# Dilated 3x3 convolution: TensorE's third to eighth pair of images as a loop of six turns, and a smaller tail of the last load in five transfers

## The chip, the cores and the metric

The kernel runs on one core of one Trainium2 chip. The metric is the device time of one execution in microseconds (us), the median of several runs. A core has five engines that each follow their own list of instructions: TensorE (PE, matrix products; its weight loads are listed as PEld), VectorE (DVE), ScalarE (ACT), GpSimd (POOL) and SyncE (SP). They meet through semaphores. Data moves between the chip's memory (HBM) and the on-chip memory (SBUF) by 16 DMA engines, which work off queues: here SP issues transfers on one (q1, hardware_dynamic) and POOL on another (q0, software_dynamic). The instructions of an engine are themselves loaded from memory through a queue of their own (q8, instruction).

## The reference

Sixteen images of 64 channels and 64 x 64 points are convolved with 128 filters of 3 x 3 taps that lie two points apart (dilation 2), with a border of zeros. All is float32.

```python
batch, c_in, h, w, c_out, k, dilation = 16, 64, 64, 64, 128, 3, 2
x_pad = np.pad(x, ((0, 0), (0, 0), (pad, pad), (pad, pad)), mode='constant')
...
output[b, co] += weight[co, ci, kh, kw] * x_pad[b, ci, kh*dilation:kh*dilation+h, kw*dilation:kw*dilation+w]
```

The output is 33.55 MB, the input 16.8 MB.

## The kernel before

**Tiling.** Two images make a pair (`pb` = 0 to 7): the 64 channels of the first lie on partitions 0 to 63, those of the second on 64 to 127, and each image uses its own half of TensorE's rows (`tile_position` 0 or 64, the loop over `hb`). A pair's 64 rows are cut into four units (`u`) of 16 output rows, and units go two at a time (`units`; the first pair starts with single ones). Input is held as float16 in `x16`, six buffers of one pair each (`pb % NX`); the output pair is gathered in `obuf`, three buffers (`pb % NO`), as float32.

**Arithmetic.** Rows are taken in groups of four: two even ones (e = 0) and two odd ones (e = 1), so that a vertical step of the dilated filter joins neighbouring groups. POOL adds the two halves of each group into `s16` (three buffers, `prepare`, L244). For each pair of units TensorE runs three phases (`phase`, L302): the middle row of taps on the sums `s16` (w1), then one phase for e = 0 (differences w21 and taps w0) and one for e = 1 (taps w2 and differences w01). ACT copies the result of the first phase out of PSUM into `s32` (L361), and DVE adds it to the results of the other two and writes the output rows (L391); for one unit in two of the last phase ACT copies PSUM out first (L387). So a tap row is multiplied fewer times than in the plain sum.

**Order on TensorE.** `phase` lists the products of two units so that a weight which both need is loaded once and used twice. `product` (L147) writes one weight load (`ldweights`, L150) when the weight is fresh, and one matmul (L152). From the second pair on, one pair is 120 matmuls (at most 64 x 512 elements each) and 68 weight loads; all eight pairs are written out one after the other. A product that must wait carries the semaphore wait itself, on its weight load, or on its matmul where the weight is already there: for the sums (POOL), and for PSUM that DVE or ACT has still to read (`free`). Where one instruction needs two waits, one of them becomes an instruction of its own. `Queue.after` leaves out a wait that an earlier one already covers.

**Loads and stores.** The first two pairs are loaded by SP as float32 and cast on the chip. The other six are cast by the transfer itself and issued by POOL (`load`, L167, transfers at L176). The last load (pair 7) is cut: partitions 0 to 111 in one transfer, the first 30 rows of the last 16 partitions in a second, and their last 34 rows in five small ones of 4, 3, 3, 3 and 3 partitions. SP stores each finished pair (L427): one transfer of 4 MB up to pair 5, two of 2 MB for pair 6, and four of 1 MB for pair 7, half a pair after each two units. The program ends when the last stores have landed (L434, L436).

```python
            if pb + 1 < NP:
                parts = [(0, P, 0, H)]
            else:
                cut, p1 = H - 34, P - 16
                parts = [(0, p1, 0, H), (p1, P, 0, cut), (p1, p1 + 4, cut, H)]
                parts += [(p, p + 3, cut, H) for p in range(p1 + 4, P, 3)]
```

Of the kernel before, what the change touches and what calls it, by code (L numbers as in the profile page):

```python
# [6 lines left out]


class Track:


    def __init__(self, tc, name, unit=1):
        self.sem, self.unit, self.n, self.known = tc.alloc_semaphore(name), unit, 0, {}
# [8 lines left out]
class Queue:  # L22
# [5 lines left out]
    def after(self, inst, *events):  # L28
        for track, n in sorted(events, key=lambda event: -len(event[0].known[event[1]])):
            if n > self.seen.get(track, 0):  # L30
                inst.wait_op(track.sem, n, "sem-ge", check=False)
                for other, m in [*track.known[n].items(), (track, n)]:
                    self.seen[other] = max(m, self.seen.get(other, 0))
        return inst


@with_exitstack
def kernel(
# [7 lines left out]
    nc = tc.nc  # L46

    B, CI, H, W = x.shape
# [5 lines left out]
    P = 128  # L54
    f32 = mybir.dt.float32
    f16 = mybir.dt.float16
    NP = B // 2
    NK = KH * KW
    NQ = H // 4
# [7 lines left out]
    NS = len(SLOT)  # L67
    NX, NSUM, NO, NP32, NPS, NR = 6, 3, 3, 4, 4, 2
    AHEAD = 5

    out_pair = out.rearrange("(nb two) c h w -> nb c two h w", two=2)
    x_pair = x.rearrange("(nb two) c h w -> nb (two c) h w", two=2)

    def sbuf(name, shape, dtype):
        return nc.alloc_sbuf_tensor(name, shape, dtype).ap()
# [4 lines left out]
    ident = sbuf("ident", [P, P], f16)  # L80
    w16 = sbuf("w16", [CO, NS * KW, 2, CI], f16)
    w_sb = sbuf("w_sb", [P, NS * KW, CO], f16)
    x16 = [sbuf(f"x16_{i}", [P, H, W], f16) for i in range(NX)]
    s16 = [sbuf(f"s16_{i}", [P, 2 * NQ, W], f16) for i in range(NSUM)]
    s32_all = sbuf("s32", [P, 2 * NP32, NB], f32)
    s32 = [s32_all[:, 2 * i : 2 * i + 2] for i in range(NP32)]
    r32 = [sbuf(f"r32_{i}", [P, 2, NB], f32) for i in range(NR)]
# [11 lines left out]
    pe, act, dve, pool, sp = (Queue() for _ in range(5))  # L99
# [3 lines left out]
    with tc.tile_critical():  # L103
# [5 lines left out]
        for track, pb, lo, hi in zip(t_x, (0, 0, 1), (0, 36, 0), (36, H, H)):  # L109
            m = nc.sync.dma_start(out=x32[pb][:, lo:hi], in_=x_pair[pb, :, lo:hi])  # L110
# [4 lines left out]
        m = nc.gpsimd.affine_select(  # L115
            out=ident,
            in_=ident,
            compare_op=mybir.AluOpType.not_equal,
            fill=1.0,
            base=0,  # L120
            pattern=[[-1, P]],
            channel_multiplier=1,
        )
# [11 lines left out]
        for n in (NB, NB, NB // 2):  # L135
            m = pe.after(
                nc.tensor.matmul(  # L137
                    out=psum[slot][:, 0, 0:n],
                    lhsT=zero[:, 0:P],
                    rhs=zero[:, 0:n],  # L140
                    start=True,
                    stop=True,
                ),
                zeroed,
            )

        def product(events, out, lhsT, rhs, start, stop, tile=None, fresh=True):  # L147
            eng = nc.tensor
            if fresh:
                m = eng.ldweights(weights=lhsT, **({"tile_position": tile} if tile else {}))  # L150
                pe.after(m, *events)
            m = eng.add_instruction(  # L152
                mybir.InstMatmult(
                    name=nc.get_next_instruction_name(),
                    ins=[eng.lower_ap(rhs), eng.lower_ap(lhsT, for_matmul_weights=True)],
                    outs=[eng.lower_ap(out)],
                    start_tensor_calc=start,
                    stop_tensor_calc=stop,
                    **({"tile_size": (CI, CO), "tile_position": tile} if tile else {}),
                    ldweights=False,  # L160
                )
            )
            return m if fresh else pe.after(m, *events)

        loaded = {}

        def load(pb, *events):  # L167
            track = t_load[(pb - 1) % len(t_load)]
            if pb + 1 < NP:
                parts = [(0, P, 0, H)]  # L170
            else:
                cut, p1 = H - 34, P - 16
                parts = [(0, p1, 0, H), (p1, P, 0, cut), (p1, p1 + 4, cut, H)]
                parts += [(p, p + 3, cut, H) for p in range(p1 + 4, P, 3)]
            for p0, p2, lo, hi in parts:
                m = nc.gpsimd.dma_start(  # L176
                    out=x16[pb % NX][p0:p2, lo:hi], in_=x_pair[pb, p0:p2, lo:hi]
                )
                loaded[pb] = track.mark(pool.after(m, *events), pool)
# [3 lines left out]
        for u in range(2):  # L183
            m = nc.scalar.copy(out=w16[:, 0:NK, u, :], in_=w32k)  # L184
# [3 lines left out]
        for name, a in (("w21", 2), ("w01", 0)):  # L188
            for u in range(2):
                eng, queue, track = (  # L190
                    (nc.vector, dve, t_dve) if name == "w21" else (nc.gpsimd, pool, t_pool)
                )
                m = eng.tensor_sub(  # L193
                    out=w16[:, SLOT[name] * KW : (SLOT[name] + 1) * KW, u, :],
                    in0=w32k[:, a * KW : (a + 1) * KW, :],
                    in1=w32k[:, KW : 2 * KW, :],
                )
# [4 lines left out]
        for n, name in enumerate(("w1", "w21", "w0", "w01", "w2")):  # L202
            slot = psum_tile()
            k0 = SLOT[name] * KW
            for j in range(KW):
                events = [made[name], ident_in] + ([free[slot]] if free[slot] else [])
                m = product(
                    events,
                    out=psum[slot][:, 0, j * CO : (j + 1) * CO],
                    lhsT=w16[:, k0 + j, :, :].rearrange("o t i -> o (t i)"),  # L210
                    rhs=ident,
                    start=True,
                    stop=True,
                )
# [3 lines left out]
            if n % 2 == 0:  # L218
                m = dve.after(nc.vector.tensor_copy(out=dst, in_=src), turned)  # L219
                ready[name] = free[slot] = t_dve.mark(m, dve)  # L220
            else:
                m = act.after(nc.scalar.copy(out=dst, in_=src), turned)  # L222
                ready[name] = free[slot] = t_act.mark(m, act)
            if n == 0:
                m = nc.vector.tensor_copy(out=x16[0][:, 0:20], in_=x32[0][:, 0:20])
# [4 lines left out]
                out=psum[slot][:, 0], lhsT=zero[:, 0:P], rhs=zero, start=True, stop=True  # L230
# [71 lines left out]
        def phase(pb, units, own, shared, alone):  # L302
            own, shared = (
                [(name, e, shift, kw) for name, e, shift in terms for kw in KWS]
                for terms in (own, shared)
            )
            own, shared = own[:alone], shared + own[alone:]
            slots, work = [], []
            for u, weights in zip(units, (own + shared, shared + own)):
                slot = psum_tile()  # L310
                slots.append(slot)
                work.append(
                    list(zip(*(conv(pb, u, hb, psum[slot][:, hb], weights) for hb in range(2))))
                )
            n, k = len(own), len(shared)
            if len(units) == 1:
                steps = [[(0, i)] for i in range(n + k)]
            else:
                steps = [[(0, i)] for i in range(n)]
                steps += [[(0, n + i), (1, i)] for i in range(k)]  # L320
                steps += [[(1, k + i)] for i in range(n)]
            done = [None] * len(units)
            for step in steps:
                for first, (t, i) in enumerate(step):
                    for hb in range(2):
                        args, events = work[t][i][hb]
                        if i == 0 and hb == 0 and free[slots[t]]:
                            events = events + [free[slots[t]]]
                        m = product(
                            events, **args, tile=(hb * CI, 0), fresh=first == 0  # L330
                        )
                    if i == n + k - 1:
                        done[t] = t_pe.mark(m, pe)
            return list(zip(slots, done))
# [4 lines left out]
        nr, freed_r, joined = 0, [None] * NR, {}  # L339
        for pb in range(NP):  # L340
            o = obuf[pb % NO]
            ov = o.rearrange("p b (q e r) w -> p b q e (r w)", e=2, r=2)
            for units in ([(0,), (1,), (2, 3)] if pb == 0 else [(0, 1), (2, 3)]):

# [4 lines left out]
                if pb + 1 < NP:  # L349
# [9 lines left out]
                slot, i = pair[0][0], n32 % NP32  # L359
                n32 += nu  # L360
                m = nc.scalar.copy(  # L361
                    out=s32_all[:, 2 * i : 2 * (i + nu)],
                    in_=psum_all[:, 2 * slot : 2 * (slot + nu)],
                )
                events = [pair[-1][1]] + [f for f in freed32[i : i + nu] if f]
# [7 lines left out]
                for e, own, shared in (  # L373
# [6 lines left out]
                    for u, (slot, done), (i, copied) in zip(  # L380
# [3 lines left out]
                        if pb and e == 1 and u == units[-1]:  # L384
                            j = nr % NR
                            nr += 1
                            m = nc.scalar.copy(out=r32[j], in_=src)  # L387
# [3 lines left out]
                        m = nc.vector.tensor_add(  # L391
                            out=ov[:, :, u * UQ : (u + 1) * UQ, e, :],
                            in0=src.rearrange("p b (q c) -> p b q c", c=QW),
                            in1=s32[i].rearrange("p b (q c) -> p b q c", c=QW),
                        )
# [19 lines left out]
                if (u + 1) % step == 0:  # L415
# [10 lines left out]
                    for dst, src in parts:  # L426
                        m = sp.after(nc.sync.dma_start(out=dst, in_=src), *events)  # L427
                        stored[pb] = track.mark(m, sp)

        last = [stored[pb] for pb in range(NP - NO, NP)]  # L430
        last = [(track, nc.sync.to_reg(n)) for track, n in last]

# [41 lines left out]
```

## Time and profile before

| What | Value |
|---|---|
| median of 3 runs | 126.73 us (125.64 to 126.93) |
| profiled execution | 126.02 us, of which the span is 124.2 us |
| granted TensorE clock, mean over the span | 0.960 |
| TensorE busy | 105.8 us, 983 matmuls; weight loads 30.3 us, 601 |
| VectorE, ScalarE, GpSimd busy | 82.7, 54.9 and 43.8 us |
| moved by DMA | 44.44 MB in 4151 packets, 358 GB/s on average |
| HBM read and written | 17.07 MB and 33.55 MB, 408 GB/s over the span |
| the stores of 4 MB, issue to landing (median) | 21.2 us |
| the four stores of 1 MB, issue to landing (median) | 10.8 us |
| SP's wait for the last stores (L436) | 8.5 us |

The span runs from the first to the last recorded instruction; the profiled execution's own time is 1.8 us longer. Shares of busy time are averages over the span. In the slices, each digit is the busy share of one fortieth of the span (3.1 us) in tenths. The profile's records of DMA packets have a queue, a start, a duration and a size, but do not say which of the 16 DMA engines moved them. The bytes of a transfer that casts float32 to float16 are counted as written.

### The profile page before, as it was taken

The page shows a single profiled execution, that of the slowest core. Times are in us where ns is not written, and L with a number is a line of the kernel's source. Part 1 is how long each engine was busy: PE and PEld are TensorE (multiplying, and loading weights), DVE is VectorE, ACT ScalarE, POOL GpSimd, SP SyncE. Part 2 cuts the span into 40 slices and gives each one's busy share as a digit, 9 for nine tenths or more (in the row PEclk, how much of TensorE's full clock was granted, in tenths as well). Part 3 has the DMA queues.
Part 4 walks back from the last instruction along what each step waited for, and adds up shares of the span by engine and source line. Part 5 has one row for each costly group of instructions (what it writes and reads, how often), then busy time and mean ns, then how long its engine had stood idle before and what let it go on. Part 6 is the DMA issues. An engine that isn't in the chain of part 4 may idle for free.

```text
span 124.2 us, 1840 instructions
## 1 busy us (share of the span) xinstructions
PE 105.8 (85%) x983; PEld 30.3 (24%) x601; DVE 82.7 (67%) x71; ACT 54.9 (44%) x41; POOL 43.8 (35%) x32
## 2 busy tenths in 40 slices
PE   4869999999999999999999999999999999920000
PEld 2234423222222222222222222222222222200000
DVE  1470958677787778777877777999686978680000
ACT  4758349717271717171717171716262626230000
POOL 2789509990939400994092001910000000000000
PEclk9999999999999999999999999999999999999555
DMA  3999999999999999999999999999999999999992
GB/s 108 366 413 348 309 266 219 216 219 427 335 317 327 372 396 335 311 343 380 324 314 368 405 418 426 435 427 417 433 433 427 427 427 433 443 419 404 422 412 90
DMA packets 4151, 44.44 MB, mean 358 GB/s; under 512 B 544, under 2 KB 544, under 8 KB 832
## 3 DMA queue, kind: packets, MB, share of 16 engines
q1 hardware_dynamic: 3104, 38.04, 73.0%
q0 software_dynamic: 1040, 6.29, 24.3%
q8 instruction: 6, 0.10, 0.3%
q14 instruction: 1, 0.01, 0.0%
HBM read 17.07 MB, written 33.55 MB: 408 GB/s over the span
## 4 chain that ended last, share of the span: by engine, by line
PE 70%; DVE 8%; DMA 5%; ACT 3%; POOL 2%; issue 1%; SPq 0%; DVEq 0%
PE ps L152 70%; DVE o L391 8%; DMA o<-in_x_dram 5%; POOL s L250 2%; ACT r L387 2%; ACT s L361 2%; SPq L106 0%; SPq L469 0%; DVEq L391 0%; SPq L103 0%
## 5 line engine op out<-in xcount | busy, mean ns | idle before, releaser
L152 PE MATMUL ps<-x,w_sb 64*128 64x496 f16 (+3 forms) x768 | 81.6, 365 | 0.1
L391 DVE TENSOR_TENSOR o<-ps,s 128x1024 f32<-128x1024 f32 x50 | 59.5, 1221 | 21.7 <-PE ps L152 15.6
L150 PEld LDWEIGHTS <-w_sb 64*128 64x128 f16 x578 | 27.5, 94 | 73.8 <-issue 56.8
L250 POOL TENSOR_TENSOR s<-x 128x2048 f16<-128x2048 f16 x6 | 24.4, 4066 | 28.9 <-DVE o L391 17.7
L361 ACT COPY s<-ps 128x2048 f32<-128x2048 f32 (+1 forms) x17 | 30.0, 1766 | 8.4 <-PE ps L152 8.4
L387 ACT COPY r<-ps 128x1024 f32<-128x1024 f32 x14 | 14.2, 1013 | 43.1 <-PE ps L152 43.1
L152 PE MATMUL ps<-s,w_sb 64*128 64x496 f16 (+1 forms) x192 | 23.2, 371 | 1.2 <-POOL s L250 0.9
L391 DVE TENSOR_TENSOR o<-r,s 128x1024 f32<-128x1024 f32 x14 | 19.1, 1366 | 2.6 <-ACT r L387 1.7
L250 POOL TENSOR_TENSOR s<-o 128x512 f16<-128x512 f32 (+4 forms) x6 | 10.3, 1740 | 5.2 <-DMA o<-in_x_dram 5.2
L237 ACT CAST x<-o 128x1024 f16<-128x1024 f32 (+3 forms) x5 | 6.5, 1349 | 0.8 <-DMA o<-in_x_dram 0.8
L176 POOL DMA_DIRECT2D x<-in_x_dram x12 | 6.6, 554 | 0.0
L137 PE MATMUL ps<-zero 128*128 128x512 f32 (+1 forms) x6 | 4.1, 848 | 1.7 <-DVE zero L113 1.7
L184 ACT CAST w<-w 128x576 f16<-128x576 f32 x2 | 2.4, 1228 | 1.7 <-DMA w<-in_weight_dram 1.7
L193 DVE TENSOR_TENSOR w<-w 128x192 f16<-128x192 f32 x2 | 1.5, 808 | 2.3 <-DMA w<-in_weight_dram 2.3
L193 POOL TENSOR_TENSOR w<-w 128x192 f16<-128x192 f32 x2 | 2.1, 1091 | 2.4 <-DMA w<-in_weight_dram 2.4
L137 PEld LDWEIGHTS ps<-zero 128*128 128x128 f32 x6 | 1.7, 304 | 3.7 <-issue 2.0
L219 DVE CAST w_sb<-ps 128x384 f16<-128x384 f32 x3 | 1.6, 552 | 1.3 <-PE ps L152 1.3
L152 PE MATMUL ps<-ident,w 128*128 128x128 f16 x15 | 1.2, 220 | 0.7 <-ACT w L184 0.5
L184 ACT ACT_TABLE_LOAD x1 | 1.3, 1283 | 0.9 <-SPq L103 0.9
L113 DVE MEMSET zero<- 128x512 f32 x1 | 0.5, 485 | 1.1 <-SPq L103 1.1
L150 PEld LDWEIGHTS <-w 128*128 128x128 f16 x15 | 0.8, 98 | 1.2 <-ACT w L184 0.9
L222 ACT CAST w_sb<-ps 128x384 f16<-128x384 f32 x2 | 0.9, 482 | 0.6 <-PE ps L152 0.6
(9 smaller groups left out, 3.1 us busy)
## 6 DMA issues: line engine op xcount, KB each, us to landing
out_dram<-o SPq DMA_DIRECT2D x6, 4096.0 KB, 21.2
x<-in_x_dram POOLq DMA_DIRECT2D x5, 1024.0 KB, 16.5
out_dram<-o SPq DMA_DIRECT2D x2, 2048.0 KB, 11.5
out_dram<-o SPq DMA_DIRECT2D x4, 1024.0 KB, 10.8
o<-in_x_dram SPq DMA_DIRECT2D x1, 2048.0 KB, 16.3
o<-in_x_dram SPq DMA_DIRECT2D x1, 1152.0 KB, 5.8
o<-in_x_dram SPq DMA_DIRECT2D x1, 896.0 KB, 7.6
x<-in_x_dram POOLq DMA_DIRECT2D x1, 896.0 KB, 14.6
```

The lines of the kernel that those rows point to most:

```text
L137: nc.tensor.matmul(out=psum[slot][:, 0, 0:n], lhsT=zero[:, 0:P], rhs=zero[:, 0:n], start=True, stop=True,),
L150: m = eng.ldweights(weights=lhsT, **({"tile_position": tile} if tile else {}))
L152: m = eng.add_instruction(mybir.InstMatmult(name=nc.get_next_instruction_name(), ins=[eng.lower_ap(rhs), eng.lower_ap(lhsT, for_matmul_wei ...
L176: m = nc.gpsimd.dma_start(out=x16[pb % NX][p0:p2, lo:hi], in_=x_pair[pb, p0:p2, lo:hi])
L184: m = nc.scalar.copy(out=w16[:, 0:NK, u, :], in_=w32k)
L193: m = eng.tensor_sub(out=w16[:, SLOT[name] * KW : (SLOT[name] + 1) * KW, u, :], in0=w32k[:, a * KW : (a + 1) * KW, :], in1=w32k[:, KW : 2 ...
L219: m = dve.after(nc.vector.tensor_copy(out=dst, in_=src), turned)
L237: m = nc.scalar.copy(out=x16[pb][:, lo:hi], in_=x32[pb][:, lo:hi])
L250: m = nc.gpsimd.tensor_add(out=dst[:, q0:q1], in0=src[:, q0:q1, 0, :], in1=src[:, q0:q1, 1, :])
L361: m = nc.scalar.copy(out=s32_all[:, 2 * i : 2 * (i + nu)], in_=psum_all[:, 2 * slot : 2 * (slot + nu)],)
L387: m = nc.scalar.copy(out=r32[j], in_=src)
L391: m = nc.vector.tensor_add(out=ov[:, :, u * UQ : (u + 1) * UQ, e, :], in0=src.rearrange("p b (q c) -> p b q c", c=QW), in1=s32[i].rearrang ...
```

## The change

TensorE's instructions for pairs 2 to 7 are no longer written out. `product` now records them (`Step`) for `pb >= FIRST`, and afterwards the recorded lists of the six pairs, `turns`, are compared step by step: they must differ only in the buffer of the input and in the values of their waits. The list of pair 2 becomes the body of a loop of six turns on TensorE alone. What differs goes by registers: the start address of each matmul's input (`x16` and `s16` become one tensor each, so that a buffer is base plus index times size), and the value that each wait compares with, raised by a constant each turn. The address registers of a product are set eight steps (`EARLY`) before its first use, in batches of five (`EACH`); a batch is one fused instruction. Each wait is an instruction of its own ahead of the product. The loop's first instruction is placed at the head of a block of 256 instructions (`head_slot`). As built, TensorE's program is 472 instructions, the loop of 221 (120 matmuls, 68 weight loads, 11 waits, 20 fused register instructions and one single, one compare and branch), and a few behind; before, it was 1,596 in a row. The order of matmuls, and all other engines' work, stay as they were, but for one branch more on each engine.

In the last load the cut moves: the second transfer holds 44 rows of the last 16 partitions, and the five small ones hold 20.

```diff
+class Step:
+    def __init__(self, group, out, lhsT, rhs, fresh, **args):
+        self.group, self.out, self.lhsT, self.rhs = group, out, lhsT, rhs
+        self.fresh, self.args, self.waits, self.incs = fresh, args, {}, []
+
+    def wait_op(self, sem, n, op, check):
+        self.waits[sem] = n
+
+    def then_inc(self, sem, n):
+        self.incs.append((sem, n))
...
+    FIRST, EARLY, EACH = 2, 8, 5
...
-    x16 = [sbuf(f"x16_{i}", [P, H, W], f16) for i in range(NX)]
-    s16 = [sbuf(f"s16_{i}", [P, 2 * NQ, W], f16) for i in range(NSUM)]
+    x16_all = sbuf("x16", [P, NX, H, W], f16)
+    x16 = [x16_all[:, i] for i in range(NX)]
+    s16_all = sbuf("s16", [P, NSUM, 2 * NQ, W], f16)
+    s16 = [s16_all[:, i] for i in range(NSUM)]
...
+        def multiply(rhs, out, lhsT, start, stop, tile=None):
+            return nc.tensor.add_instruction(
                 mybir.InstMatmult(
                     name=nc.get_next_instruction_name(),
+                    ins=[rhs, nc.tensor.lower_ap(lhsT, for_matmul_weights=True)],
+                    outs=[nc.tensor.lower_ap(out)],
...
+        turns = []
+
+        def product(events, out, lhsT, rhs, fresh=True, pb=0, group=None, **args):
+            if pb >= FIRST:
+                m = Step(group, out, lhsT, rhs, fresh, **args)
+                turns[pb - FIRST].append(pe.after(m, *events))
+                return m
+            if fresh:
+                tile = {"tile_position": args["tile"]} if "tile" in args else {}
+                pe.after(nc.tensor.ldweights(weights=lhsT, **tile), *events)
+            m = multiply(nc.tensor.lower_ap(rhs), out, lhsT, **args)
             return m if fresh else pe.after(m, *events)
...
-                cut, p1 = H - 34, P - 16
+                cut, p1 = H - 20, P - 16
...
+        def register(value):
+            reg = eng.alloc_register(f"turn{nc.next_id()}")
+            eng.reg_mov(reg, value)
+            return reg
...
+        for k, step in enumerate(body):
+            for sem, n in step.waits.items():
+                waits[k, sem] = register(n), turns[1][k].waits[sem] - n
...
+        def advance(name):
+            i, base, n, size, start = bases[name]
+            eng.reg_add(i, i, 1)
+            eng.reg_alu(i, i, n, mybir.AluOpType.python_mod)
+            eng.reg_mul(base, i, size)
+            eng.reg_add(base, base, start)
...
+        def addresses(keys):
+            for key in keys:
+                eng.reg_add(held[key], bases[key[1]][1], key[2])
...
+        with nc.Fori(0, len(turns), engines=OrderedEngineSet([eng.engine]), head_slot={eng.engine: 0}):
+            for k, step in enumerate(body):
+                for t, batch in batches:
+                    if t in (k, k - len(body)):
+                        addresses(batch)
+                for name in turning:
+                    if final[name] == k:
+                        advance(name)
...
+                for sem in step.waits:
+                    reg, every = waits[k, sem]
+                    eng.nop(nofuse=True).wait_op(sem, reg, "sem-ge", check=False)
+                    used_up.append((reg, every))
+                if step.fresh:
+                    eng.ldweights(weights=step.lhsT, tile_position=step.args["tile"])
+                m = multiply(rhs, step.out, step.lhsT, **step.args)
+                for sem, n in step.incs:
+                    m.then_inc(sem, n)
+                if len(used_up) >= EACH or step is body[-1]:
+                    for reg, every in used_up:
+                        eng.reg_add(reg, reg, every)
+                    used_up.clear()
```

## The prediction

> **What bounds the kernel now.** I read the page first: engine shares, the 40 slices, the DMA queues.
>
> ```profile
> PE 105.8 (85%) x983; PEld 30.3 (24%) x601; DVE 82.7 (67%) x71; ACT 54.9 (44%) x41; POOL 43.8 (35%) x32
> ...
> PE   4869999999999999999999999999999999920000
> ...
> DMA  3999999999999999999999999999999999999992
> ...
> q1 hardware_dynamic: 3104, 38.04, 73.0%
> q0 software_dynamic: 1040, 6.29, 24.3%
> q8 instruction: 6, 0.10, 0.3%
> ```
>
> TensorE is full until slice 35 and then has nothing to do. The DMA engines are full from slice 2 to slice 39, and the three queues together fill 97.6% of 16 engines' span. So DMA work sets the end and TensorE comes second. Six packets of that work load instructions.
>
> Second view, the chain of waits in order of time, its end:
>
> ```profile
> 84.62 24.80 PE ps L152 x238
> ...
> 109.45 1.02 ACT r L387
> ...
> 110.49 1.23 DVE o L391
> ```
>
> The last sum is done at 111.72; the span ends at 124.2. The 12.5 us between are stores, which the chain does not show.
>
> Third, the stretches between store issues (12.37 us for one pair of images):
>
> ```profile
> core 0: us, PE busy (x) PEld busy (x) DVE busy (x) ACT busy (x) POOL busy (x), PEclk, DMA share, GB/s
> 37.05:49.42 12.37, 12.37 (x124) 3.22 (x68) 9.61 (x8) 5.76 (x5) 4.58 (x2) 1.00 1.01 353
> ...
> 86.86:99.37 12.51, 12.51 (x126) 3.40 (x70) 9.61 (x8) 5.80 (x5) 0.00 (x0) 1.00 1.00 427
> 99.37:111.75 12.38, 10.03 (x98) 2.53 (x52) 9.62 (x8) 4.73 (x4) 0.00 (x0) 1.00 1.01 429
> 111.75:123.30 11.55, 0.00 (x0) 0.00 (x0) 0.00 (x0) 0.00 (x0) 0.00 (x0) 0.61 0.85 360
> ```
>
> TensorE has no gap inside a pair, and DMA is full as well: two full resources. Which has slack, and how much, comes from the trace's packet records. From 8 to 120 us never fewer than 16 packets are in flight. The 16 parts of the last store land between 120.94 and 123.27 us, 122.11 on average: the last engine is 1.16 us behind the mean.
>
> **Slack of TensorE.** An issue reaches its first packet 1.0 us later (weights: 0.96 to 1.97). Pair 6's store is issued at 99.37, so it could start at 100.4; the last DMA engine only finishes pair 5's store at 103.41. Slack: 3.0 us, after five turns of the coming loop (pairs 2 to 6). The last half pair is issued at 111.75, could start at 112.75, and the last engine is free at 118.04: 5.3 us, after six turns. If a turn takes d longer, the end moves by the larger of 5d-3.0 and 6d-5.3; up to d = 0.60, a turn of 12.97 us, nothing moves. The leading DMA engine finishes pair 5 at 101.03, so engines go idle one by one from d = 0.13, but they are not last.
>
> **The change, part by part.**
>
> **Instruction loading.** Six 16 KB packets, at 18.75, 36.80, 52.44, 68.90, 85.40 and 101.27 us, take 0.88 to 0.96 us, and the data packet behind each takes 0.81 to 1.02 in place of 0.61 or 0.62: 5.52 + 1.81 = 7.3 us, 1.22 each. Between two of them lie 237 to 282 recorded TensorE instructions, so a packet is about 250. As built, the new program has 472 TensorE instructions, then the loop of 221, which starts at the head of a block, then a few. The first two fetches remain, and the four from 52.44 go: 4 x 1.22 / 16 = 0.31 us off the mean DMA engine (0.23 if one follows the loop).
>
> **The rows of the last load.** The sixteen partition ends shrink from 4,352 to 2,560 bytes written, the block of 16 partitions before them grows from 3,840 to 5,632. The records: 0.304 us for 3,840, 0.341 for 4,352; on that line 2,560 takes 0.21 and 5,632 takes 0.43. The 3,840 packets run side by side (66.66 to 68.60, one to an engine): +0.13 everywhere. The 4,352 packets come in chains 1.55 us apart, so three or four engines hold all sixteen, about five each: 5 x -0.13 + 0.13 = -0.52 on those. The total is unchanged; GpSimd still issues seven transfers of about 0.53.
>
> **Where the end goes.** The records don't name engines. If the last three engines (2.08 to 2.33 us behind the first) are the ones with the small transfers, they gain 0.52; if they carry a kept fetch, they lose 0.13; if everything levels out, the end is the new mean, 122.11 - 0.31 = 121.80, a gain of 1.47. Between +0.13 and -1.47 I take -0.4, near the mean's gain, since nothing shows that the lost fetches sat on the last engine.
>
> **The loop on TensorE.** A turn keeps 120 matmuls and 68 weight loads. It adds 20 fused register instructions and a single one (96 operations), 11 waits as instructions of their own, and a branch. All stand in front of matmuls on one sequencer, which now passes one instruction each 63 ns (256 in 16.1 us), held back by the array. No record shows a register operation on TensorE or a matmul with a register address. Below: zero, if the sequencer does them under the 12.37 us of array work. Above: each handled like the nearest rows, a TensorE wait (51 ns) or a register move on the other engines (29 to 43, say 40): 188 x 0.051 + 96 x 0.040 + 11 x 0.051 + 0.17 (compare and branch) = 9.59 + 3.84 + 0.56 + 0.17 = 14.16 us a turn, d = 1.79. Without the 188 at 51 ns the extras are 4.57 us and leave 7.8 for 188 instructions, 41 ns each. I take zero: matmul and weight load differ from today's in one address field, and I count them nearer to today's matmuls than to waits. Both ends stay in the range.
>
> [...]
>
> **Waits.** In before, 13 weight loads over the run were released by VectorE (5.0 us in all, 0.6 at most), yet matmuls idled 0.2 us: those releases come just in time. Now the sequencer itself stops, and behind it are the weight loads and matmuls of the new product. Restarting costs 51 ns plus up to four instructions at 51, some 0.25 us, at one or two places a turn: 0 to 0.5 us, inside the 0.60, with VectorE and the stores late by as much. Cost at nothing; without that cover it is 5 x 0.5 us against 3.0.
>
> **Once.** Sixteen register moves and the branch into the loop (about 0.8 us by the rows above) lie under queued matmuls; if not, they come out of the 3.0. The extra branch on each other engine stands behind its last work.
>
> **Sum.** -0.4 us against the profiled execution: 126.02 (span 124.2, 1.8 around it) to 125.6. That execution lies 0.71 below the median, so the median goes from 126.73 to 126.3.
>
> **The rivals.**
>
> **TensorE's sequencer becomes the bound (slower).** It decides from a turn of 12.97 us. At 14.16 the end moves by 5 x 1.79 - 3.0 = 5.9 us: 132.6 on the median. For it: the 63 ns an instruction leaves little room, and TensorE's waits take 51 ns against 17 on ACT, POOL and SP. Against it: no matmul in the records shows a sequencer limit. Chance 0.25.
>
> **The head of the loop is fetched anew each turn (slower).** A stall would be 2.4 us (weights: issue to first landing, idle engines) to 5.2 (the gate's row under load). Five of them, less 3.0: +9 to +23 us, 136 to 150. Against it: 221 instructions are less than one packet holds. Chance 0.06. [...]
>
> **The DMA engines level out (faster).** The 1.47 us from above: 125.3. For it: 1.16 us of lag to win. Against it: it needs the three last engines to gain together. Chance 0.12.
>
> **The loop saves no fetch.** If each turn's start orders the next block, fetches are 2 + 6: 2 x 1.22 / 16 = +0.15, about 126.9. Chance 0.07.
>
> **How the numbers follow.** The forecast has 0.50, at 126.3, its own range 125.4 to 127.0. One per cent (1.27 us) is about what can be told from no change here: within it lie forecast and "no fetch", 0.57; faster 0.12; slower 0.25 + 0.06 = 0.31. The range runs from 125.2 (most of the levelling) to 133 (the sequencer case at its upper rows); beyond it lie the refetch and a dearer sequencer, with what is left of the levelling 0.2.
>
> **What would show it.** Right: two or three instruction packets; pairs still 12.4 to 12.9 us apart; DMA full until 120; last store parts landing within 2 us. Sequencer case: matmuls with gaps spread evenly in pairs 2 to 7, none in 0 and 1, and DMA below full from pair 5 on. Refetch: one gap of over 2 us at each turn's start and eight or more packets. I am wrong if a turn exceeds 13 us, or if the end moves by more than 1.3 us with TensorE unchanged.

## The result, and the profile after

The changed kernel takes 129.81 us (median of 6 runs, 128.94 to 130.57), the kernel before 126.40 in the same comparison: a ratio of 1.028, 95% interval 1.022 to 1.034. It is slower, by about 3.6 us on the mean (129.87 against 126.31). The forecast was 126.3 us, less than 1% from the kernel before. An execution that takes over 1.5% more than the fastest of its kernel is left out of the ratios here and below, but not out of the medians.

The page of the profiled execution (130.03 us) first: its span, the 40 slices (engine and clock in tenths) and the queue that loads instructions.

```profile
span 128.2 us, 2050 instructions
...
PE   4998999999709999999999999999999999992000
...
PEclk9999999999985699999999999999999999999655
DMA  4999999999999999999999999999979937999994
...
q8 instruction: 3, 0.05, 0.1%
```

Three things are new. TensorE, which had no hole before, is nearly idle in one slice, the twelfth. From the slice after it its granted clock drops to about half. And DMA, full up to the end before, has a hole in slices 30 to 34, deepest in slice 33. The instruction packets did fall, from six to three.

The chain of waits in order of time (start, length, what) finds the idle slice, and the waits of TensorE (in total, times, longest) name what it waited for:

```profile
34.64 1.02 ACT r L420
35.66 0.02 issue
35.69 1.24 DVE o L424
36.92 1.85 issue
38.78 77.35 PE ps L166 x720
```

```profile
PE ps L166 <- issue: 4.2, 1, 4.2
```

"Issue" is time in which the engine waited for nothing that the profile shows, and "issue: 4.2, 1, 4.2" is one such wait of 4.2 us. It stands exactly where the loop begins: 720 matmuls are six turns of 120. The views do not count branches, but the trace records them: TensorE's branch into the loop starts at 33.42 us and takes 5,087 ns. An instruction packet starts at 36.19 and lasts 0.96, the branch ends at 38.51, the first matmul of the loop follows at 38.78.

Last, the stretches between stores:

```profile
core 0: us, PE busy (x) PEld busy (x) DVE busy (x) ACT busy (x) POOL busy (x), PEclk, DMA share, GB/s
36.94:56.42 19.48, 17.64 (x146) 8.02 (x84) 9.61 (x8) 6.78 (x5) 4.56 (x2) 0.82 1.02 348
56.42:68.79 12.37, 12.37 (x124) 4.01 (x68) 9.61 (x8) 5.76 (x5) 7.61 (x8) 1.00 1.00 376
93.59:106.08 12.49, 12.49 (x125) 4.07 (x70) 9.61 (x8) 5.78 (x5) 0.00 (x0) 1.00 0.79 338
106.08:118.44 12.36, 10.03 (x98) 3.05 (x52) 9.62 (x8) 4.72 (x4) 0.00 (x0) 1.00 0.95 402
```

The first turn takes 19.48 us in place of 12.37, the next ones 12.4 as before. So all of the loss arises in the first turn, 7.1 us of it. It has two terms. The pause is 4.5 us from matmul start to matmul start, 4.3 more than usual. The clock record stands at one half from 37.40 to 44.23 us (6.83 us); the loop ran in it from 38.78, 5.45 us at half speed, which costs 2.7. Together 7.0. The store of pair 6 is issued at 106.08, 6.7 us later than before; of that the 3.0 us of slack should absorb their share and leave 3.7: the last store lands at 127.26 in place of 123.27, 4.0 us later. The DMA hole is the DMA engines waiting for that store (share 0.79).

Theory A: the loop's head lay in a block of instructions that was not loaded when the branch came, because the straight code enters the block before it only shortly earlier; the loading then holds the branch for about 5 us, and the pause also halves the clock. The trace shows the packet inside the branch's time and the clock record behind the pause; why the block was late is a guess of mine. Rivals: any jump to a placed head is dear (B), the cut of the last load makes DMA engines late (C), the loss lies in the loop's own instructions and not in the pause (D).

### The profile page after: what moved, and what is told of

The parts are those of the page before. It is cut to its first block, busy times and chain, and to the rows that moved or that the text cites. A ratio compares the mean times of both kernels' runs of the same rounds, so it can differ in the third digit from the quotient of the medians.

```text
span 128.2 us, 2050 instructions
## 1 busy us (share of the span) xinstructions
PE 109.4 (85%) x983; PEld 40.5 (32%) x601; DVE 83.7 (65%) x71; ACT 54.9 (43%) x41; POOL 43.5 (34%) x32
## 4 chain that ended last, share of the span: by engine, by line
PE 78%; DVE 8%; ACT 3%; issue 2%; DVEq 0%; SPq 0%
PE ps L166 75%; DVE o L424 6%; PE ps L155 4%; DVE x L251 2%; ACT r L420 2%; ACT s L394 1%; DVE w_sb L245 1%; DVE zero L131 0%; DVEq L621 0%; DVEq L424 0%; SPq L121 0%
## 5 line engine op out<-in xcount | busy, mean ns | idle before, releaser
L166 PE MATMUL ps<-x,w_sb 64*128 (+3 forms) x768 | 83.6, 369 | 0.5 <-DVE w_sb L245 0.4
L573 PEld LDWEIGHTS <-w_sb 64*128 64x128 f16 x408 | 28.5, 96 | 53.0 <-issue 49.5
L166 PE MATMUL ps<-s,w_sb 64*128 (+2 forms) x192 | 25.1, 387 | 4.3 <-issue 4.2
L187 PEld LDWEIGHTS <-w_sb 64*128 64x128 f16 x170 | 8.9, 94 | 17.5 <-issue 10.6
L276 POOL TENSOR_TENSOR s<-o 128x512 f16<-128x512 f32 (+4 forms) x6 | 9.7, 1640 | 5.6 <-DMA o<-in_x_dram 5.6
L155 PE MATMUL ps<-zero 128*128 128x512 f32 (+1 forms) x6 | 4.6, 946 | 1.7 <-DVE zero L131 1.7
L251 DVE CAST x<-o 128x1280 f16<-128x1280 f32 x1 | 2.2, 2182 | 0.0
```

The source lines that it names most:

```text
L155: nc.tensor.matmul(out=psum[slot][:, 0, 0:n], lhsT=zero[:, 0:P], rhs=zero[:, 0:n], start=True, stop=True,),
L166: return nc.tensor.add_instruction(mybir.InstMatmult(name=nc.get_next_instruction_name(), ins=[rhs, nc.tensor.lower_ap(lhsT, for_matmul_we ...
L187: pe.after(nc.tensor.ldweights(weights=lhsT, **tile), *events)
L276: m = nc.gpsimd.tensor_add(out=dst[:, q0:q1], in0=src[:, q0:q1, 0, :], in1=src[:, q0:q1, 1, :])
L573: eng.ldweights(weights=step.lhsT, tile_position=step.args["tile"])
```

## The experiments

**Begin the loop one pair later.** Pair 2 is written out as well, five turns remain.

```diff
-    FIRST, EARLY, EACH = 2, 8, 5
+    FIRST, EARLY, EACH = 3, 8, 5
```

> The loop begins one pair later (five turns for pairs 3 to 7, pair 2 written out), its head still at slot 0 of a block. Theory A (the 5.1 us branch into the loop was long because the straight code had entered the block before the head only a moment earlier, so the head's block was not loaded yet): with 188 more instructions between the two, the branch takes under 0.3 us, no gap of matmuls over 0.6 us ahead of pair 3, clock 1.0 throughout, pairs 12.4 us apart, time 125.5 to 126.5. Rival B (any taken branch to a block's head drops what was loaded ahead): again a branch of about 5 us, a gap of about 4 us, a halved clock, and the end 3 to 4 us later than in the kernel before, 129 to 130.5.

126.02 us against 125.76 of the kernel before, which ran again beside each set of experiments (125.76, 125.83 and 125.86 us): ratio 1.0036 (1.0008 to 1.0064). The branch into the loop takes 301 ns, again to slot 0 of a block. The slices show no hole and a full clock:

```profile
PE   4989999999999999999999999999999999900000
...
PEclk9999999999999999999999999999999999997555
```

Rival B falls: this is a taken branch to a placed head as well. The closing branches take 212 to 246 ns.

**No placement.** The loop follows the straight code directly.

```diff
-        with nc.Fori(0, len(turns), engines=OrderedEngineSet([eng.engine]), head_slot={eng.engine: 0}):
+        with nc.Fori(0, len(turns), engines=OrderedEngineSet([eng.engine])):
```

> The loop of six turns without the placement at a block's head: it follows the straight code directly, so it is not jumped into, and its 221 instructions lie across a block boundary. Theory A: no gap at the entry. Of the turns two things are open: if both blocks stay loaded, the closing branch takes 0.3 us as now, two to four instruction packets, time 125.5 to 126.7; if only sequential loading is kept, each turn loads again, 6 to 12 packets more and a gap of 2 to 5 us at each turn's start, time 137 to 150. Rival B expects no gap at the entry either, since there is no jump; for the turns it expects the second.

126.04 us, ratio 1.0031 (1.0002 to 1.0060), two instruction packets, no gap. All six turns go at full speed without the jump. That its body crosses a block boundary, as the expectation assumed, is not shown: by the next runs the straight code ends between slots 32 and 64 of a block, and 221 instructions from there may just fit. So this run says nothing of a loop across blocks.

**Head at slot 32, and at slot 64**, in place of 0 (one number in the line above).

> The changed kernel with one number different: the loop's head at slot 32 of a block, not at slot 0. Six turns as before. Theory A says that the straight code ends a few slots into a block, so slot 32 of that same block is the next place: the branch into the loop takes under 0.3 us in place of 5.1, no gap, full clock, two instruction packets, time 125.7 to 126.3 beside 125.8 of the kernel before. Rival B (a jump to a placed head is dear in itself) says 5 us again and 129 to 130.

> The changed kernel, six turns, head of the loop at slot 64. Slot 32 still had the 5.2 us branch, so the straight code must end behind slot 32 of a block (theory A) or short of the block's end before it (theory A2: the head's block is loaded only when it is entered, and first3 was spared for another reason). Theory A: slot 64 is in the block where the straight code ends, so the branch takes under 0.4 us, no gap, full clock, 125.7 to 126.5. Theory A2 and rival B: 5 us again and 129 to 130.5.

Slot 32: 129.54 us, ratio 1.0277 (1.0220 to 1.0335), with a branch of 5,160 ns. Here theory A's guess of the place was wrong. Slot 64: 126.11 us, ratio 1.0024 (1.0000 to 1.0048), with a branch of 170 ns. The two chains of waits, slot 32 and then slot 64, at the loop's entry:

```profile
36.78 1.97 issue
38.75 76.26 PE ps L166 x720
```

```profile
23.81 85.25 PE ps L166 x823
```

With slot 64 one unbroken piece of matmuls runs from 23.81 us to the last turn. The two programs differ in where the body lies and in nothing else. What fits both is that the straight code ends behind slot 32: heads at 0 and 32 can then lie only in the next block, a head at 64 lies in the block that is running. The case for the pause was settled here: one number takes it away, and by the ratios about 3.2 us with it.

The packets show what the branch waited for. In the changed kernel, with slot 32, and with slot 32 and 34 rows (below), the second instruction packet lands at 37.15, 37.09 and 37.71 us, and the branch ends 1.35, 1.39 and 1.36 us behind it. With slot 64 the same packet lands at 37.84, and the branch is over at 33.71: it did not need it.

Slot 32 also bears out the sum of the two terms. Its pause is 4.6 us, but in the profiled execution the clock is at half for 3.41 us only (39.26 to 42.68), which costs 1.7. With the 4.4 us that the pause is longer than usual this makes 6.1, and the first turn takes 18.64 us, 6.3 more than 12.37.

**More distance ahead of the head.** 64 waits that are already fulfilled near the start of TensorE's program; loop as in the changed kernel.

```diff
+        for _ in range(64):
+            nc.tensor.nop(nofuse=True).wait_op(t_dve.sem, 1, "sem-ge", check=False)
+
         def multiply(rhs, out, lhsT, start, stop, tile=None):
```

> The changed kernel, six turns, head at slot 0, with 64 fulfilled waits more near the start of TensorE's program, under its warm-up matmuls. They move the straight code 64 instructions on, so the block before the head is entered some 4 us earlier. Theory A: the branch shrinks from 5.1 to between 0.3 and 1.5 us, the gap to under 1 us, clock 1.0, time 125.8 to 126.7. Theory A2 and rival B: unchanged, 5 us and 129 to 130.5.

The branch is down to 385 ns, as theory A said and theory A2 did not. The time was a miss: 128.54 us, ratio 1.0208 (1.0159 to 1.0257). The waits did not fit under the warm-up matmuls. TensorE's timeline (start, busy time, what, idle before):

```profile
4.39 1.91 PE L155 MATMUL ps<-zero 128*128 128x512 f32 x3
8.73 0.83 PE L169 MATMUL ps<-ident,w 128*128 128x128 f16 x12 [2.43 <-issue]
```

The weights' transposes start at 8.73 us in place of 6.24 in the changed kernel, the clock falls to half from 10.4 to 17.3 us, and the first store goes out at 29.18 in place of 25.48. So the distance cures the branch and its price was paid elsewhere. The six executions lie in two groups, 127.60 to 127.88 and 129.19 to 129.31 us; the profiled one is of the second, and what the first did differently is not shown.

**A loop across two blocks.** `FIRST` = 3 and the head at slot 128; the body of 221 instructions must cross a boundary.

> The loop of five turns (from pair 3) with its head at slot 128, so that its 221 instructions lie across a block boundary and the closing branch goes back into the block before. If TensorE keeps both blocks: closing branch 0.2 to 0.3 us each turn, no gaps, four instruction packets, 125.7 to 126.5. If the older block is dropped (the refetch rival of the prediction): a branch of about 5 us and a gap of about 4 us at each of four closings, one or two packets more each turn, time 137 or more.

126.08 us, ratio 1.0023 (0.9989 to 1.0057); closing branches of 212 to 255 ns, four instruction packets (19.11, 36.15, 49.76, 60.04 us). No turn loads the body again, so the refetch rival of the prediction falls too, for a body of two blocks. (The profiled execution, of 127.80 us, has one turn of 13.40 us, with a gap of 0.4 us behind VectorE and no long branch.) The body from slot 64 above crosses a boundary as well, with three packets in all.

**The pause without a loop.** The kernel before, with 22, 46 or 66 fulfilled waits ahead of pair 2:

```diff
+                if pb == 2 and 0 in units:
+                    for _ in range(66):
+                        nc.tensor.nop(nofuse=True).wait_op(t_act.sem, 1, "sem-ge", check=False)
+
                 nu = len(units)
```

> The kernel before with 22 fulfilled waits ahead of pair 2: a pause of matmuls of about 1 us. Theory A: the clock stays at 1.0, stores come at most 1 us later, which the slack of 3.0 us takes up: the same time as the kernel before within 0.3 us. If every pause on TensorE moved the end, 126.8.

> The kernel before, all written out, with 46 waits that are already fulfilled ahead of pair 2 on TensorE: about 46 x 0.11 = 5.1 us on the sequencer, as long as the branch into the loop. Theory A: matmuls pause about 4 us, the clock is halved for about 6.8 us from some 3 us into the pause, all later stores are about 7 us later, time 129 to 130.5, with no loop in the program. Rival D (the loss lies in the loop's own instructions or its instruction packets, not in the pause): a pause alone costs less than the slack, time below 127.5.

> The kernel before with 66 fulfilled waits ahead of pair 2, since 46 gave a gap of 2.7 us: about 0.08 us each, a gap of about 4.3 us, as at the entry of the loop. Theory A: clock halved in every execution for 6.8 us, the stores from pair 2 on about 7 us late, time 129 to 130 and no longer at or near 125.7 in some executions, with all of TensorE's work written out. Rival D (the loss needs the loop): under 127.5.

| fulfilled waits | pause of matmuls | clock at half | pair 2's store | time | ratio (95%) |
|---|---|---|---|---|---|
| 22 | none over the usual | no | 49.59 | 126.02 | 1.0025 (0.9994 to 1.0055) |
| 46 | 2.71 us | 3.41 us | 53.53 | 126.21 | 1.0038 (1.0000 to 1.0075) |
| 66 | 4.97 us | 6.83 us | 57.03 | 130.48 | 1.0348 (1.0284 to 1.0411) |

(Pause, clock and store are of the one profiled execution, the time is the median.) With 66 the page and the first stretch repeat the changed kernel, though every product is written out and six instruction packets are loaded:

```profile
PE   4998999999707999999999999999999999992000
...
PEclk9999999999995599999999999999999999999655
DMA  4999999999999999999999999999979957999994
...
q8 instruction: 6, 0.10, 0.3%
```

```profile
36.99:57.03 20.04, 17.73 (x146) 5.00 (x84) 9.61 (x8) 6.79 (x5) 4.56 (x2) 0.83 1.02 351
57.03:69.40 12.37, 12.37 (x124) 3.61 (x68) 9.61 (x8) 5.76 (x5) 7.60 (x8) 1.00 0.98 360
```

So the pause alone makes the loss, and rival D falls. The run with 46 missed its expectation (129 to 130.5). A wait did cost 0.11 us, as that expectation had it, and not the 0.08 that the next one took: the waits run from 31.70 to 36.90 us, and 20 more of them lengthen the pause by 2.26 us. What was missed is that matmuls already queued ran until 34.57, over the first 2.9 us of the waits. With 22 they cover all of it, and the pause of about 1 us that was expected did not come.

The run with 46 also separates the second term from the first: a pause of 2.7 us is within the slack, so without the clock the end would not move. The profiled execution has the half clock and takes 127.29 us. The ten executions fall apart: five of 125.67 to 125.93 us with a mean clock of 0.960 to 0.965, and five of 126.48 to 127.41 with 0.947 to 0.951. Only one was profiled, so it is by these groups that a pause of this length seems to halve the clock in some executions and not in others; where it does not, the slack swallows it whole.

**The cut of the last load**, alone in the kernel before (20 rows for 34), and undone in the loop without a pause (`FIRST` = 3) and with one (slot 32):

```diff
-                cut, p1 = H - 34, P - 16
+                cut, p1 = H - 20, P - 16
```

> The kernel before with only the last load changed (20 rows in the five small transfers, not 34). Theory A: this part does nothing that can be told, 126.0 to 126.9, six instruction packets; at most the last part of the last store lands 0.5 us earlier or 0.5 us later. Rival C (the smaller tail makes some DMA engines late, and that is part of the loss): 127.5 or more.

> first3 (five turns, no stall, three instruction packets) with the last load cut at 34 rows as in the kernel before. If 20 rows suits three packets better: 0.2 to 0.6 us slower than first3, the last store's parts wider apart than its 2.4 us; if the cut does not matter: the same within 0.3 us.

> Slot 32 as in the run beside it, and the last load cut as in the kernel before (34 rows by the five small transfers). If the cut of 20 suits the fewer instruction packets: 0 to 0.5 us slower than slot32; if the cut makes no difference, as in rows20: the same within 0.3 us.

Alone: 125.75 us, ratio 1.0000 (0.9969 to 1.0031). The loop with 34 rows: 126.01 us, ratio 1.0033 (1.0003 to 1.0063), where it was 1.0036 with 20. Slot 32 with 34 rows: 130.36 us, 1.0296 (1.0232 to 1.0360), beside 1.0277 with 20. In none of the three pairs can the cut be told; rival C falls.

No run beat the kernel before. The five loops without a pause (begun at pair 3 with either cut or with the head at slot 128, unplaced, and slot 64) stand at ratios of 1.0023 to 1.0036.

## Why the prediction was wrong

**The step that failed** is the one called "Once": "Sixteen register moves and the branch into the loop (about 0.8 us by the rows above) lie under queued matmuls". The moves did: they run from 31.73 to 33.36 us, while matmuls ran until 34.6. The branch did not. It took 5.09 us in place of the 0.17 of a compare and branch, and only some 1.2 us of queued matmuls lay over it. I priced the branch by its one row in the trace of before, 168 ns at the start of the program, and did not ask whether its target would be loaded. The step's own way out, 0.8 us taken from the slack of 3.0, was short as well: the stores came 7 us late.

**The rival that came nearest** was the refetch of the head, with a stall of 2.4 to 5.2 us. The size was right at its upper row, and the place was wrong: I tied it to the closing branch of each turn, at 0.06, and never to the entry, although I wrote that the head stands at the start of a block and that 472 instructions come before. That count alone would not have given the place: 472 from a block's start end at slot 216 of the 256 that `head_slot` counts (from the first to the last instruction packet of before lie 1,259 recorded TensorE instructions, 252 to a packet), and slots 32 and 64 put the end between them. At the entry the branch took 5.09 us in the changed kernel, and 0.17 to 0.39 in the runs with slot 64, with pair 2 written out and with 64 waits more.

**A term that was missing.** No step asked what a pause does to TensorE's clock. It cost 2.7 of the 7.0 us in the profiled execution. Without it the pause would have been 4.3 us against 3.0 of slack, about 1.3 at the end. What a pause did is in the clock records: half-clock stretches of 3.41 us (slot 32, 46 waits) and 6.83 (the changed kernel, 66 waits), one twice the other, and in the changed kernel stretches of full clock of 30.72 and 75.09 us between two changes, nine and twenty-two times the shorter one. A pause of 2.71 us (46 waits) was enough in its profiled execution, and in the changed kernel the clock fell 2.8 us after the last matmul had ended (34.60 to 37.40).

**Slack of TensorE: right to 0.3 us.** 3.0 us after pair 6 was read from the packet records; the delay there of 6.7 us became 4.0 at the end. With slot 32, 46 waits and 66 waits, delays of 5.6, 4.0 and 7.3 us became 2.9, 1.3 and 4.5. So the slack was 2.7 to 2.8 in all four.

**The loop on TensorE: right in the value taken.** Zero a turn: 12.36 to 12.49 us. The upper bound of 14.16 was far off, and no run shows the dearer sequencer that lay beyond the range. After the long branch the sequencer passed 58 instructions in 1.57 us (38.51 to 40.08), five waits and five fused register instructions among them: 27 ns each, where a pair of images in before takes 66 (12.37 us for 188 matmuls and weight loads). A fused one takes 42 to 131 ns, 70 on average over 121, for what I had priced at five moves of 40.

**Waits: right.** With slot 64, matmuls start less than 0.3 us apart all through the turns.

**Instruction loading: right at its own place, not at the end.** Three packets, one following the loop's entry, where I gave two or three. The mean over the 16 engines of the last store's end (the last small packet of each, some 0.35 us ahead of its landing) is 121.76, 121.62 and 121.91 us in the three written-out kernels without a pause, and 121.39, 121.45, 121.49 and 121.43 in four loops without one (begun at pair 3 with either cut, slot 64, unplaced; the profiled execution with slot 128 took 127.80 us and is not among them): 121.76 against 121.44, 0.32 us earlier, where 0.23 was worked out for three packets fewer and 0.31 for four. But the last engine ends at 122.73 us on average in the written-out kernels and at 122.93 in the loops. **Where the end goes** is the second step that failed: I passed the gain of the mean on to the last engine, with -0.4 us. The mean fell and the last one did not; the times show no gain either, with ratios of 1.0023 to 1.0036. Why the last engine did not follow the mean is open, since the records do not name engines and these are single executions.

**The rows of the last load: right**, in that no gain or loss was put on it beyond the last engines; not even that can be told.

**The chances.** Slower had 0.31, 0.25 of it for the sequencer, whose 132.6 us stood for turns of 14.16. The range reached up to 133 for that case, which did not happen; that it held 129.81 was luck.

## What to carry to other kernels

Look for a loop's cost at its entry as well as in its turns; here the first turn lost 7.1 us and the others nothing. Find out where in its block the straight code ends, and place the head in that block (slot 64: 170 ns for the branch, slot 32: 5,160), or let more instructions run ahead of the jump. Here 64 more were enough for the branch (385 ns), and so were pair 2's 188 (301 ns). Price each pause of TensorE twice, once as time and once as the clock that it may halve (here 4.3 and 2.7 us), and compare the sum with the slack at the place where the delay is consumed (2.7 to 2.8 us). Count no gain in the mean of the DMA engines before the last of them has it: here the mean was 0.32 us earlier, and the time no shorter.

## What the runs showed of the hardware that was not expected

The branch into the loop held TensorE's sequencer for 5.1 to 5.4 us in three kernels (5,087, 5,160 and 5,427 ns; the DMA share over it was 1.03 in the changed kernel) and ended 1.35 to 1.39 us behind the instruction packet; in three others, with the head at slot 64, a pair later or behind 64 waits more, it took 170 to 385 ns. A body placed across two blocks (slot 128) was not loaded again in later turns: four packets in all, closing branches of 212 to 255 ns. Matmuls whose input address is in a register ran at the pace of written-out ones here (12.37 us a turn), and the sequencer passed loop instructions at 27 ns each behind the long branch, where a pair in before takes 66. The half-clock stretches behind a pause lasted 3.41 us in two kernels and 6.83 in four, never between, and one followed a pause of 2.71 us.
